# mLSTM heads in a deeper schedule, with scores and states in the PSUM banks of the projections

## The chip, the core and the metric

The kernel runs on one core of one Trainium2 chip. The time is device microseconds of one execution of the whole program; the median of several executions counts. One execution is also recorded by the hardware profiler, and all rows shown come from that one.

## The reference

One layer of a hybrid diffusion backbone over 1024 latent tokens of width 1024, with 256 context tokens: a half feed-forward step, a token mixing, a second half feed-forward step, each with normalisation and conditioning (the "ada" shift, scale and gate). The token mixing is a 2-D Fourier mixing beside a bidirectional mLSTM with 4 heads of width 256. Keys and queries pass a convolution of three taps and a SiLU; one direction of one head, in chunks of 128 tokens, is

```python
def step(carry, inp):
    C, n, m = carry
    ...
    w = jnp.exp(dmat - m_t[..., None])
    a = jnp.exp(inter - m_t)
    s = jnp.einsum("bhtd,bhsd->bhts", qx, kx) * w
    num = a[..., None] * jnp.einsum("bhtd,bhde->bhte", qx, C) + jnp.einsum("bhts,bhse->bhte", s, vx)
    den = a * jnp.einsum("bhtd,bhd->bht", qx, n) + jnp.sum(s, axis=-1)
    h = num / jnp.maximum(jnp.abs(den), jnp.exp(-m_t))[..., None]
    ...
    C_new = decay[..., None, None] * C + jnp.einsum("bhsd,bhse->bhde", kx * wk[..., None], vx)
```

The context tokens give the states with which both directions start. All of it is float32.

## The kernel before

**Products.** Every large product is three matmuls (`mm3`, L144 to L153): operands are split into a high and a low part by a cast on ScalarE (L140, L145) and a subtraction on VectorE (L141, L146). A projection of 128 columns over 1024 tokens is a unit: `feat_major` (L1225) loads and splits one weight tile and runs two blocks of 512 tokens, 8 k steps of three matmuls each, into one PSUM bank a block, 48 matmuls in all.

**Banks and slots.** PSUM has 8 banks in three tags: "mm" with 4 (`mm()`), "aux" with 2 and "qc" with 2 (`aux()`). SBUF tiles are tags with a number of slots too: "m" 5, "u" 16, "t" 8, "o" 8. A tile takes a slot of its tag and gives it back after its last reader. The framework puts the instructions of each engine in an order of its own, from the order in the program, the dependences and the slots.

**Background work.** `bg` is a queue of generators, each of whose `yield`s ends a step. `tick(part)` adds `rate * part` to `credit`, at most to 8, and emits one step for each whole credit; credit also grows while `bg` is empty. `side` is a second such queue, for the ada products (`ada_rest`: loads L247, sums L251 and L253, matmuls L263 and L275 into aux tiles). In `feat_major` the tick stands ahead of the three matmuls of its k step.

**The stage of the heads** (about 1110 to 1850 us of the profile). For each head h: for even h the values of two heads (`tok_major`, all four mm banks); the projections k0 and k1, whose convolution runs on VectorE and ScalarE after the eviction (L1257 to L1263, L977 to L982); then `mlstm_head` goes into `bg` with rate 5.0; the projections q0 and q1; for h = 0 the Fourier mixing; 5 or 6 gate projections (`fill`); and `drain`, which emits what is left of the head.

**`mlstm_head`** takes 25 steps. First come two steps with key transposes (`tokens`, L1290, L1291) and the scaled keys (`state_keys`, L1139), then seven backward states, each a `state_step`: two banks, two matmuls into each (L1147) and an update of half the state on VectorE (L1152). Then it yields until q1 is there. For each of 8 chunks `weights(c)` fetches a row of gate values into tile A (r, a DMA from SP at L1316), adds and masks (L1318), takes the exponential (L1320), multiplies queries and keys into the scores S (L1323, aux), weights them (L1326), multiplies the queries with both states (L1332, qc), makes the forward state of the next chunk (`state_step`) and the normalised weights pr in tile B (L1345, L1346) and hh, the part from the states (L1348, L1349). One step later `turn(c)` transposes pr (L1355), together with `store(c - 1)` (transposes L1373, DMA to hn), and one more step later `values(c)` multiplies with the values (L1362) and normalises (L1363 to L1366).

**The context.** `ctx_states` uses `state_step` as well: 16 states, in `bg` with rate 3.0 beside the values and a gate projection of the context stage (1060 to 1110 us).

Of the kernel before, what the change touches and what calls it, by code (L numbers as in the profile page):

```python
# [12 lines left out]
AF = mybir.ActivationFunctionType  # L13
ALU = mybir.AluOpType

P = 128
# [5 lines left out]
NB = SEQ // TB  # L22
# [3 lines left out]
DH = 256  # L26
NCH = SEQ // P
# [7 lines left out]
class Kernel:  # L35
# [1106 lines left out]
    def state_step(self, kw, vaug, dec, C, new):  # L1142

        nc = self.nc
        for i in range(2):
            pt = self.aux()
            nc.tensor.matmul(pt[:, :257], kw[:, i * P : (i + 1) * P], vaug, start=True, stop=True)  # L1147
            s = slice(i * 257, (i + 1) * 257)
            if C is None:
                nc.vector.tensor_copy(new[:, s], pt[:, :257])  # L1150
            else:
                nc.vector.scalar_tensor_tensor(new[:, s], C[:, s], dec, pt[:, :257], op0=ALU.mult, op1=ALU.add)  # L1152
# [75 lines left out]
    def feat_major(self, col, u2, sink):  # L1228

        w = self.a["w_in"][0].rearrange("(k p) c -> p k c", p=P)  # L1230
        ww = self.wunit(w[:, :, col : col + P])
        ps = [self.mm() for _ in range(NB)]
        for b in range(NB):
            for k in range(ND):
                self.tick(1 / 16)
                self.mm3(ps[b], (ww[0][:, k, :], ww[1][:, k, :]), (u2[b][0][k], u2[b][1][k]), k == 0, k == ND - 1)
        sink(ps)
# [31 lines left out]
    def mlstm_head(self, h, q, k, v, gates):  # L1269

        nc = self.nc
        cols, rs, db, _ = gates
        at = lambda t, i, c: t[i][c // 4][:, (c % 4) * P : (c % 4 + 1) * P]
        col = lambda qn, c, d: cols[:, qn, c, d * 4 + h : d * 4 + h + 1]
        col2 = lambda qn, c: cols[:, qn, c, :].rearrange("p (d h) -> p d h", d=2)[:, :, h]
        st = []
        for d in range(2):
            t = self.slot("st")
            nc.sync.dma_start(t, self.cst[h * 2 + d])
            st.append(t)  # L1280
        ktok = [None] * 4
        kt = lambda c: ktok[c // 2][:, (c % 2) * 256 : (c % 2) * 256 + 256]
        va = lambda c: v[c // 2][:, (c % 2) * 257 : (c % 2) * 257 + 257]

        def tokens(c):
            if ktok[c // 2] is None:
                ktok[c // 2] = self.slot("g")
            pt = self.aux()
            for i in range(2):
                nc.tensor.transpose(pt[:, i * P : (i + 1) * P], at(k, i, c), self.ident)  # L1290
            nc.scalar.copy(kt(c), pt[:, :256])  # L1291

        Cf = st[0]
        Cb = {NCH - 1: st[1]}
        kw = {}
        tokens(NCH - 1)
        yield
        tokens(NCH - 2)
        kw[NCH - 1] = self.state_keys(kt(NCH - 1), col(0, NCH - 1, 1))
        yield  # L1300
        for c in range(NCH - 1, 0, -1):
            if c > 1:
                tokens(c - 2)
                kw[c - 1] = self.state_keys(kt(c - 1), col(0, c - 1, 1))
            Cb[c - 1] = self.slot("o")
            self.state_step(kw.pop(c), va(c), db[:, 4 + h, c : c + 1], Cb[c], Cb[c - 1])
            yield

        work = {}

        def weights(c):
            A, B = self.s512("m"), self.s512("m")
            W = A[:, :256].rearrange("p (d s) -> p d s", d=2)
            SW = A[:, 256:512].rearrange("p (d s) -> p d s", d=2)
            rv = rs.rearrange("(d h) t -> d h t", d=2)[:, h, c * P : (c + 1) * P]
            nc.sync.dma_start(W, rv.unsqueeze(0).to_broadcast([P, 2, P]))  # L1316
            for d in range(2):
                nc.vector.scalar_tensor_tensor(W[:, d, :], W[:, d, :], col(3, c, d), self.mask[:, d, :],  # L1318
                                               op0=ALU.add, op1=ALU.add)
            nc.scalar.activation(A[:, :256], A[:, :256], AF.Exp)  # L1320
            S = self.aux()
            for i in range(2):
                nc.tensor.matmul(S[:, :P], at(q, i, c), at(k, i, c), start=i == 0, stop=i == 1)  # L1323
            den = self.small([P, 12], "den", bufs=3)
            for d in range(2):
                nc.vector.scalar_tensor_tensor(SW[:, d, :], S[:, :P], 1.0, W[:, d, :], op0=ALU.mult, op1=ALU.mult,  # L1326
                                               accum_out=den[:, d : d + 1])
            qc = []
            for d, C in ((0, Cf), (1, Cb[c])):
                pt = self.aux("qc")  # L1330
                for i in range(2):
                    nc.tensor.matmul(pt[:, :257], at(q, i, c), C[:, i * 257 : (i + 1) * 257],  # L1332
                                     start=i == 0, stop=i == 1)
                nc.vector.scalar_tensor_tensor(den[:, 2 + d : 3 + d], pt[:, 256:257], col(1, c, d), den[:, d : d + 1],
                                               op0=ALU.mult, op1=ALU.add)
                qc.append(pt)
            if c < NCH - 1:
                self.state_step(kw.pop(c), va(c), db[:, h, c : c + 1], Cf, Cf)
            dn, rd, sc = den[:, 4:6], den[:, 6:8], den[:, 8:10]
            nc.vector.scalar_tensor_tensor(dn, den[:, 2:4], -1.0, den[:, 2:4], op0=ALU.mult, op1=ALU.max)  # L1340
            nc.vector.tensor_tensor(dn, dn, col2(2, c), op=ALU.max)
            nc.vector.reciprocal(rd, dn)
            nc.vector.tensor_tensor(sc, rd, col2(1, c), op=ALU.mult)
            pr = B[:, :P]
            nc.vector.tensor_scalar_mul(pr, SW[:, 1, :], rd[:, 1:2])  # L1345
            nc.vector.scalar_tensor_tensor(pr, SW[:, 0, :], rd[:, 0:1], pr, op0=ALU.mult, op1=ALU.add)  # L1346
            hh = B[:, 256:512]
            nc.scalar.activation(hh, qc[0][:, :DH], AF.Copy, scale=sc[:, 0:1])  # L1348
            nc.vector.scalar_tensor_tensor(hh, qc[1][:, :DH], sc[:, 1:2], hh, op0=ALU.mult, op1=ALU.add)  # L1349
            work[c] = A, B, den  # L1350

        def turn(c):
            A, B, den = work[c]
            pt = self.aux()
            nc.tensor.transpose(pt[:, :P], B[:, :P], self.ident)  # L1355
            nc.scalar.copy(B[:, P : 2 * P], pt[:, :P])

        def values(c):
            A, B, den = work[c]
            hh = B[:, 256:512]  # L1360
            pv = self.aux()
            nc.tensor.matmul(pv[:, :DH], B[:, P : 2 * P], va(c)[:, :DH], start=True, stop=True)  # L1362
            nc.vector.tensor_tensor(hh, pv[:, :DH], hh, op=ALU.add)  # L1363
            nc.scalar.activation(A[:, :DH], hh, AF.Square, accum_out=den[:, 10:11])
            rstd = self.rstd_of(den[:, 10:11], 1, DH)
            nc.vector.tensor_scalar_mul(hh, hh, rstd)  # L1366

        def store(c):
            A, B, den = work.pop(c)
            hh = B[:, 256:512]  # L1370
            pt = self.aux()
            for i in range(2):
                nc.tensor.transpose(pt[:, i * P : (i + 1) * P], hh[:, i * P : (i + 1) * P], self.ident)  # L1373
            hT = B[:, :256].rearrange("p (i t) -> p i t", i=2)
            for i in range(2):
                j = 64 + 2 * h + i
                nc.scalar.activation(hT[:, i, :], pt[:, i * P : (i + 1) * P], AF.Copy, scale=self.hp[:, j : j + 1])
            dst = self.hn[h * DH : (h + 1) * DH, c * P : (c + 1) * P].rearrange("(i p) t -> p i t", p=P)
            nc.sync.dma_start(dst, hT)

        while q[1] is None:
            yield
        kw[0] = self.state_keys(kt(0), col(0, 0, 0))
        for c in range(NCH + 1):
            if c < NCH:
                weights(c)
                yield
                turn(c)
            if c > 0:
                store(c - 1)  # L1390
            yield
            if c < NCH:
                values(c)
                if c + 1 < NCH - 1:
                    kw[c + 1] = self.state_keys(kt(c + 1), col(0, c + 1, 0))
                yield

# [410 lines left out]
```

## Time and profile before

| | |
| --- | --- |
| three executions, median | 2758.67 us |
| lowest and highest | 2755.25 and 2763.62 us |
| the profiled execution's own time | 2761.97 us |
| its span, first to last instruction | 2760.1 us |
| mean granted TensorE clock | 0.986 |
| TensorE busy | 2661.3 us |
| stage of the heads, 1110 to 1850 us: TensorE busy | 709.51 of 740.00 us |

The span is shorter than the time by what lies around the first and last instruction, 1.9 us. A row of the timeline has the start, the length, the engine (PE is TensorE, DVE VectorE, ACT ScalarE, SPq the queue that issues DMAs), the line, the operation, what it writes and reads, and in brackets the idle time of that engine before it with what ended it. A row of the waits has who waited for whom, the total in us, how often, and the longest. PEclk is the share of its full clock that TensorE was granted.

### The profile page before, as it was taken

How to read it: one execution, taken by the hardware profiler on the slowest of the kernel's cores; microseconds unless marked ns; L12 is line 12 of the kernel's file. 1: busy time of each engine (PE TensorE's matmuls, PEld its weight loads, DVE VectorE, ACT ScalarE, POOL GpSimd, SP SyncE). 2: the span in 40 equal slices, each digit the busy share in tenths (PEclk: the TensorE clock that was granted, in tenths of full speed). 3: DMA queues.
4: the chain of work that ended last, by engine and by line, in shares of the span. 5: the costliest groups of instructions: out<-in, count | busy, mean ns of one | idle time of the engine just before them, and what ended most of it. 6: DMA issues, size and time to landing. Idle time of an engine off the chain costs nothing.

```text
span 2760.1 us, 33923 instructions
## 1 busy us (share of the span) xinstructions
PE 2661.3 (96%) x11657; PEld 2114.7 (77%) x11657; DVE 1857.2 (67%) x3341; ACT 1106.8 (40%) x1893; POOL 100.6 (4%) x217
## 2 busy tenths in 40 slices
PE   8899999998999999999999999999999999998998
PEld 5688888776877777777777778778887788887776
DVE  5688887899786438565363674555667887863765
ACT  4543332444454337233333333433345433333552
POOL 1100000000000001000000000000001000000000
PEclk9999999999999999999999999999999999999999
DMA  9765454857686545325223452356556654536874
GB/s 300 242 206 164 155 167 133 309 190 252 210 252 211 170 134 173 102 69 155 79 77 103 133 142 77 94 150 196 181 157 210 183 169 153 168 107 198 293 247 139
DMA packets 426012, 472.51 MB, mean 171 GB/s; under 512 B 25497, under 2 KB 264642, under 8 KB 425840
## 3 DMA queue, kind: packets, MB, share of 16 engines
q1 hardware_dynamic: 424448, 468.53, 54.2%
q0 software_dynamic: 1248, 1.75, 0.2%
q8 instruction: 92, 1.51, 0.2%
q14 instruction: 80, 0.66, 0.1%
q10 hardware_dynamic: 144, 0.07, 0.0%
HBM read 373.21 MB, written 97.04 MB: 170 GB/s over the span
## 4 chain that ended last, share of the span: by engine, by line
PE 75%; DVE 9%; DMA 8%; issue 4%; ACT 2%; SPq 1%; POOL 0%; DVEq 0%; POOLq 0%; ACTq 0%
PE mm L153 67%; DMA m<-r_l 2%; PE aux L1147 2%; PE qc L1332 1%; DVE u L253 1%; DVE wl L141 1%; DVE g L146 1%; DMA ld<-in_w_ada_dram 1%; DMA ld<-h 1%; DMA u<-h 1%; DMA ld<-hn 1%; PE mm L234 1%; DMA t<-gx 0%; ACT wh L140 0%; DVE wl L146 0%
## 5 line engine op out<-in xcount | busy, mean ns | idle before, releaser
L153 PE MATMUL mm<-g,wh 128*128 128x512 f32 (+1 forms) x2552 | 839.6, 409 | 11.9 <-ACT g L145 5.0
L153 PEld LDWEIGHTS mm<-g,wh 128*128 128x128 f32 (+1 forms) x2552 | 484.2, 192 | 122.2 <-ACT wh L145 6.0
L153 PE MATMUL mm<-g,wl 128*128 128x512 f32 (+1 forms) x1276 | 510.7, 402 | 3.4 <-DVE wl L146 3.3
L153 PE MATMUL mm<-g,o 128*128 128x512 f32 x2112 | 497.7, 394 | 0.0
L153 PEld LDWEIGHTS mm<-g,o 128*128 128x128 f32 x2112 | 396.9, 188 | 93.7
L141 DVE TENSOR_TENSOR wl<-wr,wh 128x1024 fp32r<-128x1024 f32 x226 | 278.8, 1234 | 223.9 <-ACT wh L140 223.2
L140 ACT CAST wh<-wr 128x1024 fp32r<-128x1024 f32 x226 | 236.3, 1046 | 352.5 <-PE mm L153 307.3
L153 PE MATMUL mm<-wh,g 128*128 128x512 f32 x1032 | 331.2, 399 | 6.6 <-ACT g L145 3.9
L153 PEld LDWEIGHTS mm<-g,wl 128*128 128x128 f32 (+1 forms) x1276 | 243.8, 191 | 59.0 <-DVE wl L146 5.6
L153 PE MATMUL mm<-u,wh 128*128 128x512 f32 (+1 forms) x848 | 268.4, 398 | 7.5 <-DVE m L704 4.9
L153 PEld LDWEIGHTS mm<-wh,g 128*128 128x128 f32 x1032 | 194.1, 188 | 54.5 <-ACT g L145 4.1
L153 PE MATMUL mm<-wl,g 128*128 128x512 f32 x516 | 205.1, 397 | 0.0
L153 PEld LDWEIGHTS mm<-u,wh 128*128 128x128 f32 (+1 forms) x848 | 159.8, 190 | 46.0 <-DVE m L704 5.4
L153 PE MATMUL mm<-wh,u 128*128 128x512 f32 x544 | 176.4, 399 | 0.0
L153 PE MATMUL mm<-u,wl 128*128 128x512 f32 (+1 forms) x424 | 167.3, 397 | 2.3 <-DVE wl L141 2.3
L582 DVE TENSOR_TENSOR t<-mm,t 128x512 f32<-128x512 f32 x128 | 88.1, 688 | 78.8 <-PE mm L153 78.6
L146 DVE TENSOR_TENSOR g<-t,g 128x512 fp32r<-128x512 f32 x154 | 103.0, 687 | 38.9 <-ACT g L145 32.1
L153 PEld LDWEIGHTS mm<-wh,u 128*128 128x128 f32 x544 | 102.0, 188 | 22.5
L145 ACT CAST o<-wa 128x512 fp32r<-128x512 f32 x88 | 54.6, 622 | 156.0 <-PE mm L153 144.8
L145 ACT CAST wh<-wr 128x1024 fp32r<-128x1024 f32 (+1 forms) x72 | 62.5, 870 | 131.9 <-PE mm L153 55.2
L153 PEld LDWEIGHTS mm<-wl,g 128*128 128x128 f32 x516 | 97.2, 188 | 23.0 <-issue 0.7
L153 PE MATMUL mm<-wl,u 128*128 128x512 f32 x272 | 108.8, 400 | 2.1 <-DVE wl L141 2.1
(469 smaller groups left out, 3432.8 us busy)
## 6 DMA issues: line engine op xcount, KB each, us to landing
wr<-in_w_a_dram SPq DMA_DIRECT2D x124, 512.0 KB, 4.4
t<-gx SPq DMA_DIRECT2D x174, 256.0 KB, 4.0
wr<-in_w_in_dram SPq DMA_DIRECT2D x80, 512.0 KB, 3.8
wr<-in_w_b_dram SPq DMA_DIRECT2D x70, 512.0 KB, 4.5
gx<-m SPq DMA_DIRECT2D x88, 256.0 KB, 4.2
gx<-t SPq DMA_DIRECT2D x66, 256.0 KB, 4.3
ld<-in_w_ada_dram SPq DMA_DIRECT2D x64, 256.0 KB, 2.8
ld<-h SPq DMA_DIRECT2D x48, 256.0 KB, 3.8
```

Source lines behind the costliest of these rows:

```text
L140: nc.scalar.copy(hv, rv)
L141: nc.vector.tensor_tensor(lv, rv, hv.bitcast(F32), op=ALU.subtract)
L145: self.nc.scalar.copy(hi, src)
L146: self.nc.vector.tensor_tensor(lo, src, hi.bitcast(F32), op=ALU.subtract)
L153: mul = lambda x, y, start, stop: self.nc.tensor.matmul(out, x, y, start=start, stop=stop, skip_group_check=grown)
L234: nc.tensor.matmul(pt[:2, :], self.sc[:, k, :], t, start=k == 0, stop=k == ND - 1)
L253: nc.vector.scalar_tensor_tensor(acc[s], t, self.sc[:, k, s : s + 1], acc[s], op0=ALU.mult, op1=ALU.add)
L582: add = lambda o, x, y: nc.vector.tensor_tensor(o, x, y, op=ALU.add)
L1147: nc.tensor.matmul(pt[:, :257], kw[:, i * P : (i + 1) * P], vaug, start=True, stop=True)
L1332: nc.tensor.matmul(pt[:, :257], at(q, i, c), C[:, i * 257 : (i + 1) * 257], start=i == 0, stop=i == 1)
```

## The change

- `state_step` takes its two banks from mm instead of aux, for the heads and for the context.
- `feat_major` asks for the bank of a block at the start of that block, not for both at the start of the unit.
- `weights(c)` is split. `weigh(c)` has the fetch of r, L1318 and the exponential; `scores(c)` has the rest, with S in mm, and without the state step. `weigh(0)` stands ahead of the wait for q1.
- The steps of a chunk: `scores(c)`; then `state_step`, `weigh(c + 1)`, the next keys, `turn(c - 1)` and `store(c - 2)`; then `values(c - 1)`. It is 25 steps again; the last chunk's values and store come in one step.
- hh is made ahead of pr; the square's unused output goes to B, so that A is free after the scores; den has four buffers.

```diff
     def state_step(self, kw, vaug, dec, C, new):
...
-            pt = self.aux()
+            pt = self.mm()
...
     def feat_major(self, col, u2, sink):
...
-        ps = [self.mm() for _ in range(NB)]
+        ps = []
         for b in range(NB):
+            ps.append(self.mm())
             for k in range(ND):
                 self.tick(1 / 16)
                 self.mm3(ps[b], (ww[0][:, k, :], ww[1][:, k, :]), (u2[b][0][k], u2[b][1][k]), k == 0, k == ND - 1)
...
-        def weights(c):
-            A, B = self.s512("m"), self.s512("m")
+        def weigh(c):
+
+            A = decay[c] = self.s512("m")
...
             nc.scalar.activation(A[:, :256], A[:, :256], AF.Exp)
-            S = self.aux()
+
+        def scores(c):
+            A, B = decay.pop(c), self.s512("m")
...
+            S = self.mm()
...
-            den = self.small([P, 12], "den", bufs=3)
+            den = self.small([P, 12], "den", bufs=4)
...
-            if c < NCH - 1:
-                self.state_step(kw.pop(c), va(c), db[:, h, c : c + 1], Cf, Cf)
...
-            nc.scalar.activation(A[:, :DH], hh, AF.Square, accum_out=den[:, 10:11])
+            nc.scalar.activation(B[:, :DH], hh, AF.Square, accum_out=den[:, 10:11])
...
+        weigh(0)
         while q[1] is None:
             yield
         kw[0] = self.state_keys(kt(0), col(0, 0, 0))
-        for c in range(NCH + 1):
+
+        for c in range(NCH + 2):
             if c < NCH:
-                weights(c)
+                scores(c)
                 yield
-                turn(c)
-            if c > 0:
-                store(c - 1)
-            yield
-            if c < NCH:
-                values(c)
+                if c < NCH - 1:
+                    self.state_step(kw.pop(c), va(c), db[:, h, c : c + 1], Cf, Cf)
+                if c + 1 < NCH:
+                    weigh(c + 1)
                 if c + 1 < NCH - 1:
                     kw[c + 1] = self.state_keys(kt(c + 1), col(0, c + 1, 0))
-                yield
+            if 0 < c <= NCH:
+                turn(c - 1)
+            if c > 1:
+                store(c - 2)
+            yield
+            if 0 < c <= NCH:
+                values(c - 1)
+                if c < NCH:
+                    yield
```

More of the change, by code (lines that the diff above doesn't have):

```diff
@@ L1307, in mlstm_head @@
             yield
-        work = {}
-        def weights(c):
-            A, B = self.s512("m"), self.s512("m")
+        work, decay = {}, {}
+        def weigh(c):
+            A = decay[c] = self.s512("m")
             W = A[:, :256].rearrange("p (d s) -> p d s", d=2)
-            SW = A[:, 256:512].rearrange("p (d s) -> p d s", d=2)
             rv = rs.rearrange("(d h) t -> d h t", d=2)[:, h, c * P : (c + 1) * P]
@@ L1320, in weights @@
             nc.scalar.activation(A[:, :256], A[:, :256], AF.Exp)
-            S = self.aux()
+        def scores(c):
+            A, B = decay.pop(c), self.s512("m")
+            W = A[:, :256].rearrange("p (d s) -> p d s", d=2)
+            SW = A[:, 256:512].rearrange("p (d s) -> p d s", d=2)
+            S = self.mm()
             for i in range(2):
                 nc.tensor.matmul(S[:, :P], at(q, i, c), at(k, i, c), start=i == 0, stop=i == 1)
-            den = self.small([P, 12], "den", bufs=3)
+            den = self.small([P, 12], "den", bufs=4)
             for d in range(2):
@@ L1343, in weights @@
             nc.vector.tensor_tensor(sc, rd, col2(1, c), op=ALU.mult)
+            hh = B[:, 256:512]
+            nc.scalar.activation(hh, qc[0][:, :DH], AF.Copy, scale=sc[:, 0:1])
+            nc.vector.scalar_tensor_tensor(hh, qc[1][:, :DH], sc[:, 1:2], hh, op0=ALU.mult, op1=ALU.add)
             pr = B[:, :P]
@@ L1346, in weights @@
             nc.vector.scalar_tensor_tensor(pr, SW[:, 0, :], rd[:, 0:1], pr, op0=ALU.mult, op1=ALU.add)
[L1347 to L1350, printed above, removed]
+            work[c] = B, den
         def turn(c):
-            A, B, den = work[c]
+            B, den = work[c]
             pt = self.aux()
@@ L1358, in values @@
         def values(c):
-            A, B, den = work[c]
+            B, den = work[c]
             hh = B[:, 256:512]
@@ L1368, in store @@
         def store(c):
-            A, B, den = work.pop(c)
+            B, den = work.pop(c)
             hh = B[:, 256:512]
```

## The prediction, made before the changed kernel ran

> **What bounds the kernel now.** I read the page first: span, shares, and the chain that ended last.
>
> ```profile
> span 2760.1 us, 33923 instructions
> ...
> PE 2661.3 (96%) x11657; PEld 2114.7 (77%) x11657; DVE 1857.2 (67%) x3341; ACT 1106.8 (40%) x1893; POOL 100.6 (4%) x217
> ...
> PE 75%; DVE 9%; DMA 8%; issue 4%; ACT 2%; SPq 1%; POOL 0%; DVEq 0%; POOLq 0%; ACTq 0%
> ```
>
> TensorE is busy 96% of the span and carries 75% of the chain. The change removes no matmul pass, so it can only win or lose TensorE's idle time and the time run at a lowered clock. Next, the windows view for the stage of the heads, for some stretches of 10 us in it, and for the end of the context projection (columns: window, length, busy time and count of PE, PEld, DVE, ACT and POOL, granted clock, DMA share, GB/s).
>
> ```profile
> 1050.00:1110.00 60.00, 57.61 (x256) 43.49 (x255) 58.54 (x140) 36.65 (x58) 7.46 (x38) 1.00 0.60 174
> 1110.00:1850.00 740.00, 709.51 (x3184) 564.36 (x3183) 408.02 (x1121) 249.36 (x526) 27.93 (x98) 0.98 0.37 105
> ...
> 1260.00:1270.00 10.00, 8.45 (x40) 6.88 (x39) 6.98 (x20) 3.27 (x6) 1.00 (x1) 1.00 0.72 178
> 1270.00:1280.00 10.00, 7.30 (x27) 5.59 (x27) 5.33 (x14) 2.82 (x8) 0.02 (x1) 0.83 0.67 205
> ...
> 1420.00:1430.00 10.00, 7.82 (x24) 6.27 (x25) 5.32 (x22) 3.35 (x8) 0.55 (x1) 0.66 0.24 56
> ```
>
> The stage holds 740.00 - 709.51 = 30.5 us of idle TensorE, and 0.02 x 740 = 15 us lost to the clock. The waits of PE in that stage say whose they are:
>
> ```profile
> PE aux L1147 <- DVE m L1326: 13.8, 6, 4.7
> PE aux L1355 <- DVE m L1346: 5.7, 4, 2.7
> PE aux L1373 <- DVE m L1366: 5.4, 4, 2.2
> PE aux L1147 <- DVE st L1152: 1.4, 1, 1.4
> ```
>
> These four are 26.3 us: the state step (L1147) that finds no aux bank because the scores still hold one, the turn (L1355) right behind the weights it transposes, the store (L1373) behind its values, and states that queue on themselves. So all that the change aims at is 26.3 us plus about 15 us of clock, some 1.5% of the span.
>
> **What it removes.** The largest group, seen in head 1's first chunks (timeline):
>
> ```profile
> 1414.11 0.38 SPq L1316 DMA_DIRECT2D m<-r_l  x1
> 1414.13 0.47 ACT L1348 ACTIVATE m<-qc,den 128x256 f32<-128x256 f32 x1 [0.47 <-DVE den L1343]
> ...
> 1420.02 0.61 DVE L1318 SCALAR_TENSOR_TENSOR m<-m,cols_l,mask 128x128 f32<-128x128 f32 x2 [3.03 <-DMA m<-r_l]
> ...
> 1422.18 1.22 PE L1147 MATMUL aux<-u,kw 128*128 128x257 f32 x2 [3.13 <-DVE m L1326]
> ```
>
> The row of gate values for chunk 1 is fetched at 1414.11, VectorE starts on it at 1420.02, and the second half of the state step can't have a bank until the scores are read. With scores and states among four banks, that step finds one. Of 15.2 us (13.8 + 1.4) I take 11 back, since the fetch of chunk 1 stays late (weigh(1) still comes after the first scores) and a projection that wants its next bank can meet it; ends 0 and 15.2. The turn now follows one step later, so I take 5 of its 5.7; ends 0 and 5.7. Of the store's 5.4 I take 1.5, because the last chunk's values and store stand in one step with no yield between; ends 0 and 5.4. The moved Square, the fourth den buffer and hh ahead of pr cost no pass; their engines are 67% and 40% busy.
>
> The clock comes with the waits:
>
> ```profile
> 1267.92 0.48 PE L1147 MATMUL aux<-u,kw 128*128 128x257 f32 x1 [1.55 <-DVE m L1326]
> ...
> 1273.38 0.33 PE L1355 MATMUL aux<-ident,m 128*128 128x128 f32 x1 [2.69 <-DVE m L1346]
> ```
>
> After the gap of 1.55 us the clock stayed at 1.00 in its window; after 2.69 us the window shows 0.83 (1.7 us lost), after 3.13 us 0.66 (3.4 us). I take 7 of the 15 us back; ends 0 and 15. Gains: 11 + 5 + 1.5 + 7 = **24.5 us**, from 0 to 41.3.
>
> The Trainium skill ("TensorE: Matmul & The Clock Gate", the section on the HAM clock gate) has the clock fall after an idle window of about 3.4 us. The trace differs: 2.69 and 3.13 us were enough here. By the page's figure only the wait of 4.7 us would have cost clock, and an estimate from it (3 of the 7 us come back) puts the sum some 4 us higher.
>
> **What it adds: an order among the mm banks.** Tiles of one tag are given their slots in order, and nobody passes. Two places show it. First the r fetch above: chunk 1's tile A comes behind chunk 0's tile B in tag m, and its DMA leaves at 1414.11, together with the first write to B at 1414.13, though the DMA needs nothing but the slot. Other heads repeat it:
>
> ```profile
> 1612.07 0.47 ACT L1348 ACTIVATE m<-qc,den 128x256 f32<-128x256 f32 x1 [2.75 <-DVE den L1343]
> 1612.11 0.42 SPq L1316 DMA_DIRECT2D m<-r_l  x1
> ...
> 1761.25 0.47 ACT L1348 ACTIVATE m<-qc,den 128x256 f32<-128x256 f32 x1
> ...
> 1761.57 0.38 SPq L1316 DMA_DIRECT2D m<-r_l  x1
> ```
>
> Second, in PSUM: head 2's start against head 1's.
>
> ```profile
> 1371.89 0.38 PE L1290 MATMUL aux<-ident,u 128*128 128x128 f32 x2
> 1372.02 0.71 PE L153 MATMUL mm<-g,wh 128*128 128x512 f32 x2
> ...
> 1377.38 0.39 PE L153 MATMUL mm<-g,wl 128*128 128x512 f32 x1
> ...
> 1378.99 0.41 PE L1290 MATMUL aux<-ident,u 128*128 128x128 f32 x2
> ...
> 1380.49 1.08 PE L1147 MATMUL aux<-u,kw 128*128 128x257 f32 x4
> ```
>
> ```profile
> 1570.56 0.62 PE L153 MATMUL mm<-g,wh 128*128 128x512 f32 x2
> ...
> 1578.79 0.69 DVE L982 SCALAR_TENSOR_TENSOR u<-t,t 128x512 f32<-128x512 f32 x1
> ...
> 1579.58 0.39 PE L263 MATMUL aux<-rb,sel 128*2 128x512 f32 x1 [0.16 <-ACT rb L145]
> ...
> 1582.23 0.40 PE L275 MATMUL aux<-ident,b 2*128 2x2 f32 x4
> 1582.56 0.44 PE L1290 MATMUL aux<-ident,u 128*128 128x128 f32 x2
> ...
> 1584.89 1.03 PE L1147 MATMUL aux<-u,kw 128*128 128x257 f32 x4
> ```
>
> In head 1 the first key transposes run at 1371.89, just ahead of q0's first matmul: that is where the tick emits them. In head 2 they wait to 1582.56, until both aux tiles of ada_rest, which come earlier in the program, have had their first matmul (1579.58 and 1582.23).
>
> Now q0. Its loop calls tick first and mm3 after. While k0 and k1 ran nothing was in bg, so credit stands at up to 8, and the first tick emits two token steps and six backward states: 12 banks, all before q0's first matmul. In aux they stood in nobody's way; in mm they stand ahead of q0's bank. Which order counts, that of mm() or that of first use? ada_rest with tags "uuuu" asks for acc before t, and acc's first write (L251) reads t: if a tile asked for earlier but still unwritten barred the way, this could not run. So I take first use. Then moving mm() into the loop changes nothing, and block 0 of q0 waits until the twelfth state bank is taken.
>
> That wait is the latency of k1's convolution, which block 0 covers today. Head 1: from 1371.89 to the first state at 1380.49 is 8.6 us; three pairs of transposes in it take 0.8 us, leaving 7.8 idle. Head 0 is alike (1185.65 to 1194.28):
>
> ```profile
> 1185.65 0.38 PE L1290 MATMUL aux<-ident,u 128*128 128x128 f32 x2
> ...
> 1194.28 1.08 PE L1147 MATMUL aux<-u,kw 128*128 128x257 f32 x4
> ```
>
> Head 3 I take as these. Head 2's last convolution ends at 1579.5; with 1.5 us from transposes to state (1378.99 to 1380.49) that is 1581.0; q0 began near 1570.56, and 10.4 us less the transposes is some 10. Sum 3 x 7.8 + 10 = 33.4 us; ends 0 (no such order) and 37.4 (head 2 waiting to 1584.89). While the states run alone:
>
> ```profile
> L1147 PE MATMUL aux<-u,kw 128*128 128x257 f32 x224 | 63.8, 397 | 15.2 <-DVE m L1326 13.8 <-DVE st L1152 1.4
> ...
> L1139 ACT ACTIVATE kw<-g,cols_l 128x256 f32<-128x256 f32 x56 | 28.6, 511 | 67.0 <-PE aux L1147 67.0
> ...
> L1152 DVE SCALAR_TENSOR_TENSOR o<-o,db_l,aux 128x257 f32<-128x257 f32 x48 | 22.3, 482 | 14.0 <-PE aux L1147 14.0
> ```
>
> a state is two updates of 482 ns on VectorE, 0.96 us, and about as much TensorE work, so I take 1 us of idle time a head: 4; ends 0 and 12. Each idle start costs clock as the 2.69 and 3.13 us gaps did, 1.7 to 3.4 us: four times 2.5 is 10; ends 0 and 13.6. The context states use state_step too:
>
> ```profile
> L1147 PE MATMUL aux<-o,kw 128*128 128x257 f32 x64 | 18.4, 392 | 0.6 <-DVE st L1150 0.3
> ```
>
> they too would be emitted ahead of a projection, where VectorE is 58.54 of 60 us busy: 4 us; ends 0 and 10. Losses: 33.4 + 4 + 10 + 4 = **51.4 us**, from 0 to 73.
>
> **Forecast.** On the profiled run's own 2761.97 us: - 24.5 + 51.4 = +26.9, so 2788.9; the median of the runs shown (2758.67) lies 3.3 lower, so 2785.6. Own range 2765 to 2806.
>
> **Rivals.** *Banks go by the order of mm().* Then block 0 runs, and only block 1, whose mm() now comes after the states, waits. Block 0 lasts from 1372.02 to the start of its 24th matmul at 1377.38 and a step more, 5.5 us, so the idle start shrinks to 2.3 us in three heads and 4.5 in head 2, 11.4; clock 4 x 1.7 = 7; with states 4 and context 2 that is 24.4, against 24.5 gained: 2758.6, no change. For it: the ties of r and B fit both orders. Against it: ada_rest's tiles.
>
> *Projections pass the states* (faster). Nothing orders the banks; a ready matmul takes any free one, and q0 covers the convolution as now. Then the gains stand, less some 3 us for blocks that wait for a bank: 2761.97 - 21.5 - 3.3 = 2737. It decides at one point: whether q0's first matmul starts before the first state's. For it: today q0 runs ahead of emitted states. Against it: 1582.56 above.
>
> *It doesn't do what it says*: the late r fetch keeps VectorE waiting, and the 13.8 us move from L1147 to L153. That takes 11 from the gains of any case and is in the ranges.
>
> **Chances.** Forecast 0.58, order of mm() 0.22, passing 0.20. A difference of 0.3%, 8.3 us, is about what a measurement of this kernel can tell from none. Forecast: 0.53 slower, 0.05 same. Order of mm(): 0.07 faster, 0.13 same, 0.02 slower. Passing: faster. Together 0.27, 0.18, 0.55. The range runs from 2738, which leaves out half of the passing case (0.10), to 2804, which leaves out some 0.06 above.
>
> **What would show it.** Right: an idle TensorE of 7 to 10 us ahead of the first L1147 in every head, L153 waiting there, all six states before q0's first L153 with the clock lowered behind them; the turn's wait gone. Order of mm(): q0's first 24 matmuls in place and a gap of some 2 us after them. Passing: no gap at q0, and the waits on L1326 and L1346 gone. Wrong in size if L153 shows waits on L1326 in the chunks, or if L1318's wait on r grows.

## The result, and the profile after

| | median | lowest to highest | runs |
| --- | --- | --- | --- |
| before | 2758.18 us | 2755.25 to 2763.62 | 4 |
| changed | 2792.41 us | 2785.74 to 2796.76 | 4 |

The changed kernel is slower: the ratio is 1.0118 with a 95% interval of [1.0097, 1.0138], some 33 us. The profiled execution of the changed kernel has a span of 2790.5 us and a granted clock of 0.983 (before 2760.1 and 0.986). Lines from 1230 on are renumbered in it: the key transposes L1290 are L1291, the turn L1355 is L1359, values L1362 is L1366, the store L1373 is L1377.

The waits of PE in the stage of the heads (1110 to 1880 us) of the changed kernel; the columns are the total in us, the times, the longest:

```profile
PE aux L1291 <- DVE u L982: 20.1, 3, 6.7
PE aux L1377 <- DVE m L1370: 10.2, 7, 2.8
PE aux L263 <- ACT rb L145: 10.2, 2, 9.8
PE mm L1479 <- DMA ld<-z: 2.7, 5, 0.7
PE mm L1487 <- DVE acc L1485: 2.4, 4, 0.7
PE aux L1366 <- ACT m L1360: 2.3, 1, 2.3
PE qc L1338 <- ACT m L1349: 1.8, 2, 1.3
```

The two largest waits of before are gone: no state step behind L1326, no turn. In their place stand three waits of 6.7 us for a convolution (L982 writes its result) and one of 9.8 us, and the store's wait has grown from 5.4 to 10.2 us. TensorE's timeline at the start of head 1 shows the first kind:

```profile
1385.95 0.39 PE L153 MATMUL mm<-g,wl 128*128 128x512 f32 x1
1386.18 0.38 PE L1291 MATMUL aux<-ident,u 128*128 128x128 f32 x2
...
1393.26 0.69 PE L1291 MATMUL aux<-ident,u 128*128 128x128 f32 x2 [6.69 <-DVE u L982]
...
1394.89 2.06 PE L1147 MATMUL mm<-u,kw 128*128 128x257 f32 x4
...
1401.72 1.03 PE L1147 MATMUL mm<-u,kw 128*128 128x257 f32 x4
...
1402.40 0.82 PE L153 MATMUL mm<-g,wh 128*128 128x512 f32 x2
```

Before, q0's first matmul stood 0.13 us behind the first transposes (1371.89 and 1372.02). Now it stands 16.2 us behind them (1386.18 and 1402.40), and 6.69 us of that are idle. All four mm banks stand empty meanwhile: the last eviction of k1, below, ends at 1387.79, and nothing writes to one before the first state at 1394.89.

```profile
1387.11 0.68 ACT L1258 ACTIVATE wa<-mm,cc 128x512 f32<-128x512 f32 x1
```

Head 2 is the longer one:

```profile
1586.86 0.40 PE L153 MATMUL mm<-g,wl 128*128 128x512 f32 x1
...
1597.08 1.31 PE L263 MATMUL aux<-rb,sel 128*2 128x512 f32 x2 [9.82 <-ACT rb L145]
1599.06 0.58 PE L275 MATMUL aux<-ident,b 2*128 2x2 f32 x4 [0.67 <-ACT b L266]
1599.58 1.84 PE L1291 MATMUL aux<-ident,u 128*128 128x128 f32 x6
1601.36 1.20 PE L1147 MATMUL mm<-u,kw 128*128 128x257 f32 x2
```

Here the key transposes still stand behind the two aux tiles of ada_rest, and with q0 held up nothing is left for TensorE. The windows view of the changed kernel, for the end of the context projection, the stage of the heads and stretches at the heads' starts (columns as in the prediction):

```profile
1050.00:1110.00 60.00, 53.14 (x226) 40.41 (x226) 56.18 (x135) 33.72 (x52) 6.52 (x31) 0.94 0.55 165
1110.00:1880.00 770.00, 716.62 (x3217) 576.48 (x3216) 413.48 (x1119) 250.12 (x531) 27.74 (x98) 0.97 0.35 103
...
1390.00:1400.00 10.00, 6.50 (x25) 4.96 (x26) 5.29 (x10) 4.40 (x11) 0.10 (x1) 0.66 0.17 48
...
1600.00:1610.00 10.00, 10.00 (x41) 7.76 (x39) 6.51 (x15) 5.73 (x15) 0.00 (x0) 0.70 0.35 101
```

The context lost too: TensorE is busy 53.14 of 60 us against 57.61 before, at a clock of 0.94 against 1.00. Behind an idle start the clock is lowered while TensorE works: 0.70 in a stretch in which it was busy throughout.

### The profile page after: what moved, and what is told of

It reads as the page before. It is cut to its first block, busy times and chain, and to the rows that moved or that the text cites. A ratio compares the mean times of both kernels' runs of the same rounds, so it can differ in the third digit from the quotient of the medians.

```text
span 2790.5 us, 33956 instructions
## 1 busy us (share of the span) xinstructions
PE 2663.1 (95%) x11657; PEld 2125.8 (76%) x11657; DVE 1861.8 (67%) x3341; ACT 1104.9 (40%) x1893; POOL 99.4 (4%) x217
## 4 chain that ended last, share of the span: by engine, by line
PE 73%; DVE 10%; DMA 9%; issue 5%; ACT 2%; SPq 1%; POOL 0%; DVEq 0%; POOLq 0%; ACTq 0%
PE mm L153 64%; PE mm L1147 2%; DMA wr<-in_w_a_dram 2%; DVE wl L141 2%; PE qc L1338 1%; DMA m<-r_l 1%; DVE u L253 1%; ACT wh L140 1%; DMA ld<-h 1%; DMA wa<-in_w_ada_dram 1%; DVE g L146 1%; DMA u<-h 1%; PE mm L234 1%; DMA g<-in_w_b_dram 0%; DMA ld<-xT 0%
## 5 line engine op out<-in xcount | busy, mean ns | idle before, releaser
L153 PE MATMUL mm<-g,wh 128*128 128x512 f32 (+1 forms) x2552 | 822.7, 404 | 12.6 <-ACT g L145 5.0
L153 PEld LDWEIGHTS mm<-g,wh 128*128 128x128 f32 (+1 forms) x2552 | 478.7, 190 | 121.3 <-ACT g L145 5.7
L153 PE MATMUL mm<-g,wl 128*128 128x512 f32 (+1 forms) x1276 | 502.6, 396 | 4.0 <-DVE wl L146 4.0
L153 PE MATMUL mm<-g,o 128*128 128x512 f32 x2112 | 497.8, 395 | 0.0
L153 PEld LDWEIGHTS mm<-g,o 128*128 128x128 f32 x2112 | 397.6, 188 | 93.1
L153 PE MATMUL mm<-wh,g 128*128 128x512 f32 x1032 | 331.9, 400 | 5.6 <-ACT g L145 3.8
L153 PEld LDWEIGHTS mm<-g,wl 128*128 128x128 f32 (+1 forms) x1276 | 241.0, 189 | 58.7 <-DVE wl L146 5.6
L153 PE MATMUL mm<-u,wh 128*128 128x512 f32 (+1 forms) x848 | 270.5, 401 | 7.2 <-DVE m L704 4.2
L153 PEld LDWEIGHTS mm<-wh,g 128*128 128x128 f32 x1032 | 195.2, 189 | 52.8 <-ACT g L145 4.1
L153 PE MATMUL mm<-wl,g 128*128 128x512 f32 x516 | 205.7, 399 | 0.0
L153 PEld LDWEIGHTS mm<-u,wh 128*128 128x128 f32 (+1 forms) x848 | 161.4, 192 | 45.7 <-DVE m L704 4.7
L153 PE MATMUL mm<-wh,u 128*128 128x512 f32 x544 | 175.4, 398 | 0.0
L153 PE MATMUL mm<-u,wl 128*128 128x512 f32 (+1 forms) x424 | 168.6, 400 | 2.8 <-DVE wl L141 2.7
L153 PEld LDWEIGHTS mm<-wh,u 128*128 128x128 f32 x544 | 102.2, 188 | 22.5
L145 ACT CAST o<-wa 128x512 fp32r<-128x512 f32 x88 | 54.6, 622 | 157.8 <-PE mm L153 152.1
L153 PEld LDWEIGHTS mm<-wl,g 128*128 128x128 f32 x516 | 97.7, 189 | 22.8 <-issue 0.7
L153 PE MATMUL mm<-wl,u 128*128 128x512 f32 x272 | 108.2, 398 | 1.3 <-DVE wl L141 1.3
```

The source lines that it names most:

```text
L145: self.nc.scalar.copy(hi, src)
L153: mul = lambda x, y, start, stop: self.nc.tensor.matmul(out, x, y, start=start, stop=stop, skip_group_check=grown)
```

## The experiments

All are compared with the kernel before on the same chip; its median was 2756.1 us beside the first four, 2754.8 beside the next four and 2755.2 beside the last two. Beside the changed kernel it was 2758.2, so a difference between medians of different groups can hold some 3 us of such distance.

**Backward and context states back in aux.**

```diff
-    def state_step(self, kw, vaug, dec, C, new):
+    def state_step(self, kw, vaug, dec, C, new, bank=None):
...
-            pt = self.mm()
+            pt = (bank or self.mm)()
...
-            self.state_step(kw.pop(c), va(c), db[:, 4 + h, c : c + 1], Cb[c], Cb[c - 1])
+            self.state_step(kw.pop(c), va(c), db[:, 4 + h, c : c + 1], Cb[c], Cb[c - 1], self.aux)
...
-                            C if n % 2 else None, N)
+                            C if n % 2 else None, N, self.aux)
```

> The changed kernel, with the backward states of the heads and the context states put back into aux; scores and forward states stay in mm. Theory (banks of one tag are granted in order of first use, so that q0's first block waits for twelve state banks): the idle TensorE of 6.7, 6.7, 9.8 and 6.7 us ahead of the first state of each head goes, and the context's 7 us too. The heads' starts lost 38 us against before (18.9 - 3.1 and so on, after what the states leave less to do later), so 2792 - 38 - 7 = some 2747 us, 2738 to 2756. Rival (the new order of steps in the chunks, or scores in mm, is what costs): the time stays above 2775. Rival (the convolution itself ends later after the change): the gaps stay.

Measured: 2748.74 us (2743.55 to 2750.07), 0.9973 [0.9963, 0.9983] of before. So the two uses of state_step cost the change 43.7 us (2792.4 - 2748.7; 41.4 when this program was measured again, as told below), and what is left of the change is faster than before. The start of head 1 in this kernel:

```profile
1364.75 0.38 PE L1291 MATMUL aux<-ident,u 128*128 128x128 f32 x2
1364.88 0.71 PE L153 MATMUL mm<-g,wh 128*128 128x512 f32 x2
...
1371.85 0.42 PE L1291 MATMUL aux<-ident,u 128*128 128x128 f32 x2
...
1373.36 1.07 PE L1147 MATMUL aux<-u,kw 128*128 128x257 f32 x4
```

From the first transposes to the first state are 8.6 us, as before and as after the change (1386.18 to 1394.89, 8.7 us). The convolution isn't later; what changed is only whether q0 runs beside it. The states are emitted ahead of q0 here too, and q0 passes them, so their place in the program alone doesn't hold it up; their banks do.

**The matmuls ahead of the tick.**

```diff
-                self.tick(1 / 16)
                 self.mm3(ps[b], (ww[0][:, k, :], ww[1][:, k, :]), (u2[b][0][k], u2[b][1][k]), k == 0, k == ND - 1)
+                self.tick(1 / 16)
```

> The changed kernel, with the three matmuls of a k step ahead of the tick in feat_major instead of behind it, so that q0's first block has its bank before the first tick emits the states. Theory (order of first use): block 0 of q0 runs at once, block 1 still waits behind the states, so of each head's idle start about 5.5 us go and 1 to 4 stay; with the clock 2792 - 22 - 6 = some 2764 us, 2756 to 2774; the context is as after the change. Rival (the order of asking for the bank counts, or the states are simply first by priority): no change, 2792 and gaps of 6.7 us.

Measured: 2764.14 us (2757.96 to 2772.95), 1.0036 [1.0024, 1.0049] of before, 28 us less than the changed kernel. Its timeline at head 1:

```profile
1380.31 0.71 PE L153 MATMUL mm<-g,wh 128*128 128x512 f32 x2
...
1384.97 0.40 PE L153 MATMUL mm<-g,wl 128*128 128x512 f32 x1
1386.57 0.44 PE L1291 MATMUL aux<-ident,u 128*128 128x128 f32 x2 [1.20 <-DVE u L982]
...
1388.04 1.13 PE L1147 MATMUL mm<-u,kw 128*128 128x257 f32 x4
```

Block 0 runs through, its last matmul at 1384.97, and then TensorE stops for 1.20 us, because block 1 still stands behind the states. What the edit does to q0 is to put block 0's first use ahead of the burst. It moves the matmuls of every other projection too, and not all of the 28 us are q0's: in the context stage, 1050 to 1110 us, the clock is 1.00 again (0.94 in the changed kernel), and the states wait 2.1 us for L1011 instead of 5.2.

**Both banks asked for at the top again.**

```diff
-        ps = []
+        ps = [self.mm() for _ in range(NB)]
         for b in range(NB):
-            ps.append(self.mm())
```

> The changed kernel, with both banks of a projection asked for at its top again, as before. Theory (order of first use): when mm() is called does not matter, so the same gaps of 6.7 us and 2792 us within the scatter (2785 to 2797). Rival (order of mm() calls): both banks stand ahead of the states, q0 runs through, and the time falls to some 2745.

Measured: one run of 2783.62 us, 2 us under the lowest of the changed kernel, with gaps of 6.70, 6.69, 10.98 and 6.70 us. Every engine has its instructions in the very order of the changed kernel, so this part of the change does nothing at all; the 9 us between this run and the other's median are scatter.

**Only the deeper schedule.**

```diff
-            pt = self.mm()
+            pt = self.aux()
...
-            S = self.mm()
+            S = self.aux()
```

> Only the deeper schedule: scores and all states in aux as before, the rest as after the change. Theory: no idle start; the turn's 5.7 us are gone, the state step still waits for the scores' aux bank (some 10 to 15 us), so some 2752 us, 2744 to 2760. Rival (the new order of steps costs by itself): above 2765.

Measured: 2758.80 us, 1.0013 [1.0003, 1.0024]. Its largest waits of PE in the stage:

```profile
PE aux L1359 <- DVE st L1152: 11.2, 8, 3.0
PE aux L1377 <- DVE m L1370: 7.7, 6, 2.4
PE mm L1487 <- DVE acc L1485: 4.8, 2, 3.3
```

The turn no longer waits for its weights (5.7 us before), but for an aux bank that a state holds: 11.2 us. The state step's wait of 13.8 us behind the scores, expected to stay, is gone as well. All listed waits of PE in the stage add up to 29.9 us, against 30.5 before. The schedule alone wins nothing.

**Scores in mm, all states in aux**, in the deeper schedule.

```diff
-            pt = self.mm()
+            pt = self.aux()
             nc.tensor.matmul(pt[:, :257], kw[:, i * P : (i + 1) * P], vaug, start=True, stop=True)
```

> Deeper schedule, scores in mm, all states in aux. Tells where the 7 us come from that the kernel with backward states in aux wins over before. If the scores' bank alone mattered (the 13.8 us of L1147 behind L1326), it is as good as that kernel: 2746 to 2752 us. If forward states have to leave aux as well, because the turn then waits for a state's bank (11.2 us of L1359 behind L1152 with all in aux), it is 2752 to 2760.

Measured: 2758.91 us, 1.0021 [1.0012, 1.0030]. The turn waits 11.6 us for a state's bank, as with all in aux; the listed waits add up to 28.9 us. The first experiment differs from this one in the forward states' place, and in that of nothing else, and is faster: it is the forward states that have to leave aux.

**Forward states in mm in the old schedule**, the kernel before otherwise.

```diff
-    def state_step(self, kw, vaug, dec, C, new):
+    def state_step(self, kw, vaug, dec, C, new, bank=None):
...
-            pt = self.aux()
+            pt = (bank or self.aux)()
...
-                self.state_step(kw.pop(c), va(c), db[:, h, c : c + 1], Cf, Cf)
+                self.state_step(kw.pop(c), va(c), db[:, h, c : c + 1], Cf, Cf, self.mm)
```

> The kernel before with one edit: the forward states of the chunks in mm; no deeper schedule, scores in aux. The 15.2 us of L1147 go, the turn's 5.7 us stay: if idle time comes back one to one with half of its clock, some 2740 us; if it is given back elsewhere as in the kernel with backward states in aux (20.9 us of waits gone, 14.5 us of others new), 2748 to 2756.

Measured: 2754.87 us, 0.9995 [0.9985, 1.0005]. Its largest waits:

```profile
PE aux L1355 <- DVE m L1346: 16.6, 10, 2.9
PE aux L1373 <- DVE m L1366: 4.7, 4, 1.8
PE aux L1362 <- ACT m L1356: 2.9, 1, 2.9
```

The 15.2 us of the state step are gone, and the turn waits 16.6 us instead of 5.7: the chain behind the chunk's gate row is late as ever, and the next instruction that needs it now does the waiting. The listed waits add up to 29.6 us.

**Credit 0 ahead of a head**, with scores and states in mm as in the change.

```diff
+            self.credit = 0.0
             self.later(self.mlstm_head(h, q, k, v[h % 2], gates), rate=5.0)
```

> The changed kernel, with credit set to 0 before a head is put into bg, so that its first steps are emitted one by one over q0 and q1 and not eight at q0's first tick. Theory (order of first use): scores and states stay in mm, but both blocks of q0 have their first matmul ahead of nearly all states, so the gaps of 6.7 and 9.8 us ahead of q0 go, while the context keeps its 7 us: 2792 - 38 = some 2754 us, 2747 to 2762. Rival (states in mm slow the projections by sharing the four banks, whenever they are emitted): above 2770.

Measured: 2749.88 us, 0.9986 [0.9977, 0.9996], 42 us less than the changed kernel. Its start of head 1:

```profile
1381.24 0.27 PE L1291 MATMUL aux<-ident,u 128*128 128x128 f32 x1
1381.27 0.71 PE L153 MATMUL mm<-g,wh 128*128 128x512 f32 x2
...
1387.80 1.07 PE L1147 MATMUL mm<-u,kw 128*128 128x257 f32 x4
1388.52 0.58 PE L153 MATMUL mm<-g,wh 128*128 128x512 f32 x1
```

The gaps at q0 are gone, though every state of the heads is still in mm. So it is not sharing the four banks that costs, but that twelve of them were asked for in one burst ahead of q0.

**No drain between heads**, on the kernel with backward and context states in aux.

```diff
-            self.drain()
             if h == HEADS - 1:
+                self.drain()
```

> The kernel with backward and context states in aux, and without the drain between heads: the last steps of a head are emitted beside the next head's k projections or values. If the rest of the gain is lost in the tails, where store waits for values with nothing beside it (L1377 behind L1370, 9.5 us, most of it at head ends), some 5 to 9 us with the clock come back: 2739 to 2745. If the tails are covered anyway, no change: 2749.

Measured: 2750.96 us, 0.9986 [0.9973, 0.9999], with the store's wait at 9.3 us. A miss: the order of the instructions is that of the kernel without this edit, since a head's 25 steps are all emitted by the end of its gate projections, and the drain finds nothing. As it is one program measured on two chips (0.9973 and 0.9986), it says how far such ratios can be trusted: some 3 or 4 us. The store's waits at the heads' ends stay untested.

**Credit 0, and the context states in aux.** The edit is credit 0 and the one line of `ctx_states` from the first experiment.

> The changed kernel with credit set to 0 ahead of each head and the context states in aux; scores and all states of the heads stay in mm. Theory: against the kernel with credit 0 alone (2749.9) only the context's cost goes, idle 8.1 to some 1 us between 1050 and 1110 and up to 5 us of clock there: 2739 to 2745 us. Rival (the context's wait is made up behind it, since the profile's gap there is followed by a stage with slack): 2747 to 2751.

Measured: 2741.59 us (2739.89 to 2746.36), 0.9952 [0.9935, 0.9969]: the lowest of all, some 14 us under before and 51 under the changed kernel. Against credit 0 alone it is 8.3 us by the medians of two chips, the price of the context states in mm. Its windows:

```profile
1050.00:1110.00 60.00, 59.09 (x263) 45.24 (x262) 58.38 (x146) 33.94 (x54) 5.99 (x30) 1.00 0.63 185
1110.00:1880.00 770.00, 746.35 (x3386) 599.04 (x3385) 432.70 (x1138) 263.99 (x545) 26.88 (x98) 1.00 0.38 112
```

**Backward and context states in aux, and credit 0.**

> Backward and context states in aux as in the first experiment, and credit 0 ahead of each head as well. If the burst of eight steps costs only through the banks of mm, it is as good as without credit 0: 2745 to 2752 us. If emitting later also delays the chunks, so that less is covered at the head's end, 2752 to 2760.

Measured: 2743.73 us (2739.30 to 2748.95), 0.9959 [0.9942, 0.9975]. It is faster than the same without credit 0 (0.9973), a little beyond what was expected, and by an amount that two measurements of one program also differ by; whether a spread start helps by itself stays open.

## Why the prediction was right

**The order of the banks was right, and so was its rule.** The prediction took it from the r fetch that leaves with the first write to B, and from head 2's transposes behind two unwritten aux tiles; it chose first use over the order of mm() because ada_rest asks for acc before t. The run with both banks at the top shows that the call's place does nothing, the run with the matmuls ahead of the tick that the place of the first use decides whether block 0 runs. The rival by order of mm() would have kept block 0 running; it stood still. The rival in which projections pass the states falls with the same rows.

**The idle starts**: 33.4 us forecast, 6.70 + 6.69 + 9.82 + 6.70 = 29.9 found. The latency was right (8.6 us forecast, 8.7 found in head 1), but what was not that one gap, transposes and a second gap of 0.25 us, took 2.0 us of it (8.7 - 6.69) where 0.8 was taken off.

**States alone**: 1 us of idle time a head was taken. In head 1 the six states run from 1394.89 to 1402.40, 1.25 us each, at a granted clock of 0.50 up to 1397; TensorE has hardly a gap there, so this term was next to nothing.

**The clock behind the idle starts**: 10 us forecast. In the first 10 us behind each start the granted clock was 0.80, 0.77, 0.55 and 0.69, which is 2.0 + 2.3 + 4.5 + 3.1 = 11.9 us:

```profile
1195.86:1205.86 10.00, 9.75 (x42) 7.72 (x42) 3.87 (x9) 5.01 (x13) 0.00 (x0) 0.80 0.00 0
1393.26:1403.26 10.00, 9.75 (x41) 7.76 (x42) 5.53 (x12) 6.07 (x16) 0.00 (x0) 0.77 0.00 0
1597.08:1607.08 10.00, 9.19 (x31) 6.18 (x32) 5.67 (x12) 4.07 (x11) 0.00 (x0) 0.55 0.38 108
1750.00:1760.00 10.00, 9.75 (x39) 7.63 (x39) 4.72 (x11) 5.54 (x15) 0.00 (x0) 0.69 0.00 0
```

**The context was mis-sized**: 4 us forecast, 8.3 found, inside the ends of 0 and 10. The windows of the changed kernel agree: 57.61 - 53.14 = 4.5 us of idle time and 0.06 x 60 = 3.6 us of clock. The gap lies where the values' eviction is late, in the changed kernel's timeline:

```profile
1094.29 0.39 PE L153 MATMUL mm<-wh,u 128*128 128x512 f32 x1
1097.85 1.63 PE L1147 MATMUL mm<-o,kw 128*128 128x257 f32 x3 [3.17 <-DVE o L1011]
```

The next projection stands behind the states of heads 2 and 3, which need the values that L1011 still has to write.

**The sum of losses**, 51.4 us, was near: the first experiment puts it at 43.7 by the medians, and at 48.8 by the spans of the two profiled executions (2790.5 - 2741.7).

**The gains were mis-sized**, 24.5 us forecast and 7.4 found (2756.1 to 2748.7 in the first experiment; 3.8 when its program was measured again as "no drain", 13.6 in the best version). The forecast was right that the state step's and the turn's waits would go; it failed in letting them come back as time. The store, of which it wanted 1.5 us back, lost instead: 9.5 us in the first experiment against 5.4. In the first experiment 13.8 + 1.4 + 5.7 = 20.9 us of waits are gone. The store's grew by 4.1; values (L1366), the queries times the states (L1338) and the Fourier mixing (L1479, L1487; L1467 and L1475 before, 1.2 and 1.1 us) wait for 8.6 us more, and smaller ones for some 1.5. That gives back 14 of the 20.9: all listed waits of the stage fall from 30.5 to 23.8 us. The term for the clock was about right: the mean granted clock of the first experiment's executions is 0.9913, against 0.9892 in those of before beside it, and by an estimate from these two (0.0021 of 2750 us) 6 us of the 7.4 are clock, where 7 were forecast. So of the 17.5 us of waits that were to come back, 1 to 7 did, by the medians less the clock or by the list of waits.

```profile
PE aux L1377 <- DVE m L1370: 9.5, 8, 2.4
PE mm L1479 <- DMA ld<-z: 2.5, 4, 0.7
PE mm L1487 <- DVE acc L1485: 2.4, 4, 0.7
PE aux L1366 <- ACT m L1360: 2.3, 2, 1.8
PE qc L1338 <- ACT m L1349: 2.3, 2, 1.5
```

The prediction itself said that the row of gate values stays late. It did: VectorE's wait for it, the first row before and the second in the first experiment, is hardly shorter. That this is why the waits move on along the chunk is likely, but no run fetched the row earlier.

```profile
DVE m L1318 <- DMA m<-r_l: 54.6, 24, 5.1
DVE m L1319 <- DMA m<-r_l: 49.9, 21, 5.1
```

The three partial versions say the same from the other side: each removes waits in full and is no faster, because another instruction of the same chunk takes them over; in all three the listed waits stay within 2 us of the 30.5 before. Of the versions tried, only those with scores, forward states and schedule together win anything; forward states and schedule without the scores, and scores and forward states in the old schedule, were not tried. The forecast and the outcome lie 7 us apart (2785.6 and 2792.4) since both sides were too large, the gains by 17 us and the losses by 8; the rest is the distance between medians of different chips. That the sum came out so close is luck in part: two errors that cancel.

**What it said the profile would show** held but for the name of the waiting line: not L153 but L1291 and L263 carry the wait, being the next in TensorE's order. L153 shows up only by being absent. Of its two signs of a wrong size neither appeared, so they did not catch the gains: L153 shows no wait on the scores in the chunks, and VectorE's wait for r did not grow (54.6 us before, 48.6 in the changed kernel).

## What to carry to other kernels

Before moving a tile to another tag, ask what is emitted ahead of what: where slots are granted in order of first use, as here, a burst of background work that takes slots of the main work's tag stops the main work, however free the banks are. Spreading the burst (42 us here, for one line) was as good as moving the tile (43.7). And a wait listed at one line is not time to be won: first find what the next instruction of the same chain will wait for.

## What the runs showed of the hardware

The clock can fall after idle times of less than 3 us, but their length alone doesn't decide: in the kernel before, 2.69 us of idle TensorE was followed by a stretch at 0.83, 1.55 us by none, and in the changed kernel 2.85 us were followed by a stretch at 1.00 (a row of the timeline and one of the windows):

```profile
1870.07 0.44 PE L1377 MATMUL aux<-ident,m 128*128 128x128 f32 x2 [2.85 <-DVE m L1370]
...
1870.00:1880.00 10.00, 9.51 (x43) 7.59 (x44) 6.44 (x13) 5.23 (x11) 0.55 (x1) 1.00 0.61 199
```

It also comes back slowly enough to matter: behind the 9.82 us in head 2, a stretch in which TensorE was busy for all of its 10 us was granted 0.70, 3 us lost.
